# Where tiles start in SBUF: moving every TensorE operand to a multiple of 256 bytes

## The chip, the cores and the metric

The kernel runs on one core of a Trainium2 chip. The metric is the device time of one execution in microseconds (us), as the median of several runs. TensorE (PE) multiplies; its weight loads are shown as a row of their own (PEld). VectorE is DVE, ScalarE is ACT, GpSimd is POOL, and SyncE (SP) issues the DMAs. SBUF is the on-chip memory that all engines read; an address below is an offset in bytes within a partition of SBUF.

## The reference

An encoder of four layers works on 256 tokens of width 1024. Layer i has one token mixer (i mod 3), then a dense SwiGLU layer; each half is normalised before and after.

```
for i in range(4):
    hn = rmsnorm(x, norm_w[i, 0])
    m = [retention, conv_module, dilated_attention][i % 3](hn, ...)
    x = x + rmsnorm(m, norm_w[i, 1])
    a = rmsnorm(x, norm_w[i, 2]) @ ffn_w_in[i]            # 1024 -> 2 * 2816
    x = x + rmsnorm((silu(a[:, :2816]) * a[:, 2816:]) @ ffn_w_out[i], norm_w[i, 3])
```

So the mixers are retention, conv, attention and retention again. Nearly all the arithmetic is products of a 256-token activation with a weight matrix in float32.

## The kernel before

The tokens are held as two tiles of 128 (t = 0 and t = 1). Each float32 factor of a product is split in two parts of type float32r, a high part `h` and the rest `l`, and a product is made of three matmuls: h·h, h·l and l·h. A weight block of 128 x 1024 arrives by DMA in `raw`; ACT casts it to `wh` (L50) and DVE makes `wl` by a subtraction (L51). Ten such pairs rotate in the pool `wp`.

`proj` (L181) multiplies an activation with four weight blocks: 24 matmuls into one PSUM bank. The *moving* operand, the one that streams through the array, is a 512-column slice of `wh` or `wl` (384 columns in attention). The *stationary* operand, which a weight load puts into the array beforehand, is a 128-column block of the transposed activation, `xTh0`/`xTl0` for t = 0 and `xTh1`/`xTl1` for t = 1. Every matmul comes with its own weight load.

`out_block` (L198; L188 in its other order) makes the products with an output matrix. In the SwiGLU layer its moving operands are `poolh`/`pooll` and its stationary ones `fhh`/`fhl`; in retention they are `wh`/`wl` and `rh`/`rl`. `mix` of retention (L322) has `vh`/`vl` moving and `ph`/`pl` stationary. `taps` of the conv layer (L575) multiplies 256 columns of `upad` with diagonal blocks `dg` in plain float32. Transposes (L160, L457, L693 and others) are PE instructions too.

The SwiGLU layer goes through 11 groups of 256 hidden columns. For group c the order on PE is up(0, c+1), down(0, c), a transpose, up(1, c), down(1, c-1), a transpose, where up is `proj` and down is 12 matmuls of `out_block`.

Where a tile lies is not written anywhere in the code. Pools take space one behind the other in the order of the code, and each tile starts at the next multiple of 32 bytes after the one before. A tile of 4 or 8 bytes per partition thus moves all that lies behind it by 32 bytes. The small tiles ahead of and between the large ones are `nhalf` (4 bytes), two pairs of `rsx` (8 bytes each), six `ss`, six `rs`, `bn`, `lnm`, `asc` and `warm`.

Of the kernel before, what the change touches and what calls it, by code (L numbers as in the profile page):

```python
# [8 lines left out]
F32 = mybir.dt.float32  # L9
F32R = mybir.dt.float32r  # L10
AF = mybir.ActivationFunctionType
# [3 lines left out]
P = 128  # L15
D = 1024
KB = 8
# [3 lines left out]
PAIRS = 8  # L21
# [16 lines left out]
def tile_trunk(ctx: ExitStack, tc: tile.TileContext, a):  # L38
    nc = tc.nc

    const = ctx.enter_context(tc.tile_pool(name="const", bufs=1))
    wp = ctx.enter_context(tc.tile_pool(name="wp", bufs=WBUFS))
    work = ctx.enter_context(tc.tile_pool(name="work", bufs=2))
# [32 lines left out]
        with tc.issue_after(cast[0].ins), tc.issue_after(cast[1].ins):  # L76
            yield

# [1 line left out]
    xs = [const.tile([P, D], F32, tag=f"x{t}", name=f"x{t}") for t in range(2)]  # L80
    grow = work.tile([1, D], F32, tag="gain", name="grow", bufs=2)
    nc.sync.dma_start(grow, a["norm_w"][0:1, :])
# [6 lines left out]
    gain0 = [bank("acc"), bank("acc")]  # L89
    for hh in range(2):  # L90
        nc.tensor.matmul(gain0[hh], lhsT=ones, rhs=grow[:, hh * 512 : hh * 512 + 512], start=True, stop=True)
    nhalf = const.tile([P, 1], F32, tag="nhalf", name="nhalf")
    nc.vector.memset(nhalf, -0.5)

    xTh, xTl = [None, None], [None, None]

# [5 lines left out]
    def rsqrt_mean(ss0, ss1, eps, scale=None, keep=None):  # L102
        if keep is None:
            r = work.tile([P, 2], F32, tag="rs", name="rs", bufs=6)
        else:
            r = const.tile([P, 2], F32, tag=f"rsx{keep}", name="rsx", bufs=2)
        if scale is None:
            nc.gpsimd.tensor_scalar(r[:, 0:1], ss0, ss1, eps, op0=ALU.add, op1=ALU.add)  # L108
        else:
            nc.gpsimd.tensor_scalar(r[:, 0:1], ss0, scale, eps, op0=ALU.mult, op1=ALU.add)  # L110
        nc.gpsimd.tensor_tensor(out=r[:, 1:2], in0=r[:, 0:1], in1=nhalf, op=ALU.pow)
        return r[:, 1:2]
# [20 lines left out]
    rsx = {}  # L133
# [69 lines left out]
                    stop=(last and i == 2),  # L203
                )

# [1 line left out]
    def retention_decay(j, pool):  # L207
        tmp = pool
        dist = work.tile([P, 2, 512], F32, tag="fg", name="dist", bufs=1)
        nc.sync.dma_start(dist, a["ret_dist"])  # L210
        lm = tmp.tile([P, 8], F32, tag="lm", name="lm")
        nc.sync.dma_start(lm, a["log1m"][j : j + 1, :].partition_broadcast(P))
        ebase = tmp.tile([P, 8], F32, tag="ebase", name="ebase")
        nc.vector.memset(ebase, math.e)
        ex = tmp.tile([P, 8], F32, tag="ex", name="ex")
        nc.gpsimd.tensor_tensor(out=ex, in0=ebase, in1=lm, op=ALU.pow)
        gm = tmp.tile([P, 8], F32, tag="gm", name="gm")
        nc.vector.tensor_scalar(gm, ex, -1.0, 1.0, op0=ALU.mult, op1=ALU.add)
        lg = tmp.tile([P, 8], F32, tag="lg", name="lg")
        nc.scalar.activation(lg, gm, AF.Ln)  # L220
        dts = []
        for h in range(RET_HEADS):
            dt = pool.tile([P, 512], F32, tag=f"dt{j}_{h}", name=f"dt{j}_{h}", bufs=1)
            nc.vector.tensor_scalar_mul(dt, dist[:, 0, :], lg[:, h : h + 1])
            nc.vector.scalar_tensor_tensor(
                out=dt, in0=dist[:, 1, :], scalar=lg[:, 4 + h : 5 + h], in1=dt, op0=ALU.mult, op1=ALU.add
            )
            nc.scalar.activation(dt, dt, AF.Exp)
            dts.append(dt)
        return dts  # L230

# [1 line left out]
    def retention(j, gload, decay, finish, pool, first):  # L233
        dts = []
        rope = pool.tile([P, 2, 2, P], F32, tag="rope", name="rope", bufs=1)
# [274 lines left out]
        finish(1, acc[1])  # L510

    def conv(j, finish, pool, prefetch):
        chv = pool.tile([P, 5, KB], F32, tag="chv", name="chv", bufs=1)
        nc.sync.dma_start(chv, a["conv_ch"][j])
        wdw = pool.tile([P, KB, TAPS], F32, tag="wdw", name="wdw", bufs=1)
        nc.sync.dma_start(wdw, a["conv_w_dw"][j])
        bout = pool.tile([P, D], F32, tag="cbout", name="cbout", bufs=1)
# [4 lines left out]
        cvp = pool.tile([P, KB, 256], F32, tag="cvp", name="cvp", bufs=1)  # L522

        def perm(v):
            # natural token 4 u + r, read as (r, u)
            return v.rearrange("p (u r) -> p r u", r=4)

        def glu(t, c, ws, mid=None):
# [74 lines left out]
        with tc.issue_after(last_tap["v"].ins):  # L603
            wo = [load_w(a["conv_w_out"][j, k]) for k in range(CONV_EARLY)]
        yh, yl = {}, {}
        warm = pool.tile([P, 1], F32, tag="warm", name="warm", bufs=1)
        with tc.issue_after(last_tap["a"].ins):
            nc.scalar.activation(warm, nhalf, AF.Silu)
        for t in range(2):
            bs = [bank("acc"), bank("acc")]  # L610
            bn = work.tile([P, 2, 6], F32, tag="bn", name="bn", bufs=2)
            ms = work.tile([P, 4], F32, tag="lnm", name="lnm", bufs=2)
            for hh in range(2):
                for k in range(4):
                    nc.tensor.transpose(
                        bs[hh][:, k * P : (k + 1) * P], cvp[:, 4 * hh + k, t * P : (t + 1) * P], ident
                    )
                nc.vector.bn_stats(bn[:, hh, :], bs[hh])
            nc.vector.bn_aggr(ms[:, 0:2], bn)
            rs = rsqrt_mean(ms[:, 1:2], None, LN_EPS, scale=1.0)  # L620
            nc.vector.tensor_scalar(ms[:, 2:3], ms[:, 0:1], rs, -1.0, op0=ALU.mult, op1=ALU.mult)
            yc = pool.tile([P, D], F32, tag="yc", name="yc", bufs=1)
            nc.vector.tensor_scalar(yc[:, 0:512], bs[0], ms[:, 0:1], rs, op0=ALU.subtract, op1=ALU.mult)
            nc.scalar.activation(yc[:, 512:1024], bs[1], AF.Identity, scale=rs, bias=ms[:, 2:3])
            h = const.tile([P, KB, P], F32R, tag=f"xTh{t}", name=f"yh{t}")
            l = const.tile([P, KB, P], F32R, tag=f"xTl{t}", name=f"yl{t}")
            for hh in range(2):
                tp = bank("aux")
                sy = pool.tile([P, 4, P], F32, tag="sy", name="sy", bufs=2)
                for k in range(4):  # L630
                    cb = 4 * hh + k
                    nc.tensor.transpose(tp[:, k * P : (k + 1) * P], yc[:, cb * P : (cb + 1) * P], ident)
                for k in range(4):
                    cb = 4 * hh + k
                    nc.scalar.activation(
                        sy[:, k, :],
                        tp[:, k * P : (k + 1) * P],
                        AF.Silu,
                        scale=chv[:, 1, cb : cb + 1],
                        bias=chv[:, 2, cb : cb + 1],  # L640
                    )
                ends = split(
                    h[:, 4 * hh : 4 * hh + 4, :].rearrange("p k t -> p (k t)"),
                    l[:, 4 * hh : 4 * hh + 4, :].rearrange("p k t -> p (k t)"),
                    sy.rearrange("p k t -> p (k t)"),
                )
                if t == 0 and hh == CONV_FENCE:
                    with tc.issue_after(ends[0].ins), tc.issue_after(ends[1].ins):
                        wo += [load_w(a["conv_w_out"][j, k]) for k in range(CONV_EARLY, KB)]
                        prefetch()  # L650
            yh[t], yl[t] = h, l
# [191 lines left out]
        outp(1, range(4, KB))  # L843
        finish(1, acc[1])

# [1 line left out]
    pre_norm(0, gain0, late=True)  # L847

    for i in range(DEPTH):
        kind, j = i % 3, i // 3  # L850
        gains = {}

        def finish(t, f):
            post_norm(t, f, gains[0])
            pre_norm(t, gains[1])
# [27 lines left out]
            ffn(i, finish_ffn, pool)  # L883


# [1 line left out]
def _layout(inputs):  # L887
    import numpy as np

    f32 = np.float32  # L890
    pos = np.arange(256)
    tok = 4 * (pos % 64) + pos // 64
# [10 lines left out]
    w = inputs["ret_w_in"]  # L903
    nr = w.shape[0]
    qk = w[:, :, : 2 * D].reshape(nr, D, 2, RET_HEADS, 256).transpose(0, 3, 1, 2, 4).reshape(nr, RET_HEADS, 1, D, 512)
    vg = w[:, :, 2 * D :].reshape(nr, D, 2, RET_HEADS, 512).transpose(0, 3, 2, 1, 4)
    w = np.concatenate([qk, vg], axis=2)
# [4 lines left out]
    w = inputs["conv_w_in"]  # L912
    n = w.shape[0]
# [4 lines left out]
    chv = [inputs[k].reshape(n, 1, KB, P) for k in ("conv_b_dw", "conv_ln_g", "conv_ln_b")]  # L918
# [3 lines left out]
    c["conv_b_out"] = inputs["conv_b_out"]  # L922
    w = inputs["attn_w_in"]
    n = w.shape[0]
    w = w.reshape(n, D, 3, 3, PAIRS, 2, 64)  # group, qkv, pair, head of pair, dim
    qk = w[:, :, :, 0:2].transpose(0, 4, 3, 1, 5, 2, 6)  # n pair qk D head group dim
    g0 = qk[:, :, :, :, :, 0].reshape(n, PAIRS, 2, D, 128)
    g12 = qk[:, :, :, :, :, 1:3].reshape(n, PAIRS, 2, D, 256)
    qk = np.concatenate([g0, g12], axis=4)
    v = w[:, :, :, 2].transpose(0, 3, 1, 2, 4, 5).reshape(n, PAIRS, 1, D, 384)  # L930
    w = np.concatenate([qk, v], axis=2)
# [1 line left out]
        w.reshape(n, PAIRS, 3, 4, 2, P, 384).transpose(0, 1, 2, 3, 5, 4, 6).reshape(n, PAIRS, 3, 4, P, 768)  # L933
    )
    c["attn_w_out"] = inputs["attn_w_out"].reshape(n, KB, P, D)
    # tables of positions only
    tf = tok.astype(f32)
    diff = tok[None, :] - tok[:, None]  # query n minus key m, [m, n]
    dist = np.stack([np.maximum(diff, 0), np.maximum(-diff, 0)]).astype(f32)  # 2, m, n
    c["ret_dist"] = dist.reshape(2, 2, P, 256).transpose(2, 0, 1, 3).reshape(P, 2, 512)  # L940
    inv = (1.0 / (f32(10000.0) ** np.linspace(0.0, 1.0, 128, dtype=f32))).astype(f32)
    ang = tf[:, None] * inv[None, :]
# [36 lines left out]
```

## Time and profile before

| | |
|---|---|
| median of three runs | 1625.04 us (1624.56 to 1625.5) |
| span of the profiled execution, first to last instruction | 1623.5 us |
| PE busy | 1604.0 us (99%), 7742 matmuls and transposes |
| PEld busy | 1345.9 us |
| DVE busy | 1038.4 us (64%) |
| ACT busy | 864.0 us (53%) |
| DMA | 274 MB, mean 169 GB/s |
| mean granted TensorE clock | 0.997 of full speed (2.4 GHz) |

The profiled execution has no time of its own beside its span; the median of the timed runs is 1.5 us longer than the span, which is what lies around the first and last instruction. Matmuls are pipelined, so the busy time of PE says only that it never ran dry. How fast it goes is read from the distance between the starts of two matmuls that follow each other.

### The profile page before, as it was taken

Reading aid. Unit: us, or ns where it says so; the run is one execution under the profiler, and the core shown is the slowest. Engines: PE = TensorE matmul, PEld = TensorE weight load, DVE = VectorE, ACT = ScalarE, POOL = GpSimd, SP = SyncE. Lnnn points to the kernel's source line nnn. Section 1 sums busy time; section 2 is a strip of 40 time slices with the busy share of each in tenths; the row PEclk is TensorE's granted clock in tenths of the full one; section 3 lists DMA queues with packets and bytes.
Section 4 is the critical chain, followed back from the end, with each engine's and each line's share of the span. In section 5 each row is a group of like instructions: output and inputs, shape, how many; then the busy total and the mean of one; then the engine's idle time right before and its main releaser. Section 6 shows DMA issues by size and latency. Waiting matters only on the chain.

```text
span 1623.5 us, 20999 instructions
## 1 busy us (share of the span) xinstructions
PE 1604.0 (99%) x7742; PEld 1345.9 (83%) x7742; DVE 1038.4 (64%) x1576; ACT 864.0 (53%) x1376; POOL 69.8 (4%) x106
## 2 busy tenths in 40 slices
PE   9999999999999999999999999999999999999998
PEld 6888878888787788889999999788888888878886
DVE  7755685546797854557777767755567655675452
ACT  7544464445687644546656656644456444555341
POOL 1000010001000100010000000100010000010000
PEclk9999999999999999999999999999999999999999
DMA  8645474655304755544444444564655543475530
GB/s 316 234 137 178 156 244 171 203 185 182 121 1 145 254 200 179 169 131 142 153 147 131 143 143 156 202 213 168 205 174 169 180 167 127 160 238 194 194 117 26
DMA packets 79882, 274.27 MB, mean 169 GB/s; under 512 B 9378, under 2 KB 9634, under 8 KB 79779
## 3 DMA queue, kind: packets, MB, share of 16 engines
q1 hardware_dynamic: 79778, 272.92, 49.7%
q8 instruction: 61, 1.00, 0.2%
q14 instruction: 43, 0.34, 0.1%
HBM read 271.84 MB, written 1.05 MB: 168 GB/s over the span
## 4 chain that ended last, share of the span: by engine, by line
PE 91%; DVE 3%; ACT 2%; DMA 2%; issue 1%; POOL 0%; SPq 0%; DVEq 0%; POOLq 0%; ACTq 0%
PE mm L181 58%; PE acc L198 20%; PE acc L575 3%; PE aux L322 1%; PE acc L772 1%; PE aux L457 1%; DMA raw<-in_ffn_w_out 1%; PE acc L731 1%; PE acc L729 1%; PE aux L757 1%; DVE wl L51 1%; ACT junk L116 1%; PE aux L298 1%; DMA raw<-in_ffn_w_in 1%; PE aux L693 1%
## 5 line engine op out<-in xcount | busy, mean ns | idle before, releaser
L181 PE MATMUL mm<-wh,xTh 128*128 128x512 f32 (+1 forms) x1536 | 596.8, 389 | 0.8 <-ACT xTh L50 0.8
L181 PE MATMUL mm<-wh,xTl 128*128 128x512 f32 (+1 forms) x1536 | 583.1, 380 | 0.0
L181 PE MATMUL mm<-wl,xTh 128*128 128x512 f32 (+1 forms) x1536 | 582.6, 379 | 0.0
L51 DVE TENSOR_TENSOR wl<-raw,wh 128x1024 fp32r<-128x1024 f32 (+1 forms) x432 | 497.5, 1163 | 118.9 <-ACT wh L50 107.9
L50 ACT CAST wh<-raw 128x1024 fp32r<-128x1024 f32 (+1 forms) x432 | 429.1, 1003 | 141.7 <-PE mm L181 107.8
L181 PEld LDWEIGHTS mm<-wh,xTl 128*128 128x128 f32 x1536 | 289.1, 188 | 50.2 <-DVE xTl L51 0.3
L181 PEld LDWEIGHTS mm<-wl,xTh 128*128 128x128 f32 x1536 | 289.8, 189 | 44.5 <-DVE wl L51 0.5
L181 PEld LDWEIGHTS mm<-wh,xTh 128*128 128x128 f32 x1536 | 289.3, 188 | 44.8 <-ACT xTh L50 1.2
L446 ACT ACTIVATE fsg<-mm,rsx 128x256 f32<-128x256 f32 x88 | 41.7, 473 | 171.6 <-PE mm L181 171.6
L448 DVE SCALAR_TENSOR_TENSOR fsg<-mm,rsx,fsg 128x256 f32<-128x256 f32 x88 | 42.3, 481 | 127.7 <-ACT fsg L446 127.5
L51 DVE TENSOR_TENSOR pooll<-raw,poolh 128x1024 fp32r<-128x1024 f32 x88 | 107.4, 1222 | 9.2 <-ACT poolh L50 7.9
L198 PE MATMUL acc<-poolh,fhh 128*128 128x512 f32 x344 | 108.6, 396 | 0.5 <-ACT fhh L50 0.5
L198 PE MATMUL acc<-poolh,fhl 128*128 128x512 f32 x344 | 107.3, 392 | 0.0
L198 PE MATMUL acc<-pooll,fhh 128*128 128x512 f32 x344 | 107.1, 393 | 0.0
L50 ACT CAST poolh<-raw 128x1024 fp32r<-128x1024 f32 x88 | 92.2, 1049 | 26.7 <-PE acc L198 15.4
L51 DVE TENSOR_TENSOR fhl<-aux,fhh 128x256 fp32r<-128x256 f32 x88 | 37.0, 421 | 98.4 <-ACT fhh L50 98.4
L50 ACT CAST fhh<-aux 128x256 fp32r<-128x256 f32 x88 | 32.5, 369 | 115.6 <-PE aux L457 115.6
L198 PEld LDWEIGHTS acc<-pooll,fhh 128*128 128x128 f32 x344 | 64.6, 188 | 14.5
L198 PEld LDWEIGHTS acc<-poolh,fhh 128*128 128x128 f32 x344 | 63.7, 188 | 15.4 <-ACT fhh L50 2.7
L198 PEld LDWEIGHTS acc<-poolh,fhl 128*128 128x128 f32 x344 | 64.3, 188 | 14.6
L559 DVE SCALAR_TENSOR_TENSOR cv<-upad,wdw,cv 128x256 f32<-128x256 f32 x143 | 59.5, 479 | 0.8
L108 POOL TENSOR_SCALAR rs<-ss 128x1 f32<-128x1 f32 x16 | 7.5, 468 | 1061.5 <-ACT junk L116 1061.5
(178 smaller groups left out, 1617.2 us busy)
## 6 DMA issues: line engine op xcount, KB each, us to landing
raw<-in_ffn_w_in SPq DMA_DIRECT2D x176, 512.0 KB, 4.8
raw<-in_ret_w_in SPq DMA_DIRECT2D x96, 512.0 KB, 4.6
raw<-in_ffn_w_out SPq DMA_DIRECT2D x88, 512.0 KB, 4.4
raw<-in_attn_w_in SPq DMA_DIRECT2D x96, 384.0 KB, 3.7
raw<-in_ret_w_out SPq DMA_DIRECT2D x32, 512.0 KB, 4.7
raw<-in_conv_w_in SPq DMA_DIRECT2D x16, 512.0 KB, 4.6
gain<-in_norm_w SPq DMA_DIRECT2D x15, 512.0 KB, 5.2
raw<-in_conv_w_out SPq DMA_DIRECT2D x8, 512.0 KB, 4.0
```

The source lines that it names most:

```text
L50: ia = nc.scalar.copy(h, src)
L51: iv = nc.vector.tensor_sub(l, src, h.bitcast(F32))
L116: nc.scalar.activation(junk, src, AF.Square, scale=scale, accum_out=acc)
L181: nc.tensor.matmul(out, lhsT=st[t][:, k, :], rhs=mv[:, sl], start=(n == 0), stop=(n == 23))
L198: nc.tensor.matmul(acc[hh], lhsT=st, rhs=mv[:, hh * 512 : hh * 512 + 512], start=(first and i == 0), stop=(last and i == 2),)
L298: nc.tensor.matmul(b[:, m * 256 : (m + 1) * 256], lhsT=kt[:, 2 + half, m * P : (m + 1) * P], rhs=qt[:, half, :], start=(n == 0), stop=(n = ...
L322: nc.tensor.matmul(b, lhsT=pt[:, m, t * P : (t + 1) * P], rhs=vt[:, m, :], start=(n == 0), stop=(n == 5))
L446: nc.scalar.activation(sg, b[:, 0:256], AF.Silu, scale=rsx[t])
L448: nc.vector.scalar_tensor_tensor(out=sm, in0=b[:, 256:512], scalar=rsx[t], in1=sg, op0=ALU.mult, op1=ALU.mult)
L457: nc.tensor.transpose(tp[:, k * P : (k + 1) * P], sm[:, k * P : (k + 1) * P], ident)
L559: last_tap["v"] = nc.vector.scalar_tensor_tensor(out=cv, in0=upad[:, cb, w : w + 256], scalar=wdw[:, cb, w : w + 1], in1=cv, op0=ALU.mult, ...
L575: nc.tensor.matmul(pc[:, 0:256], lhsT=dgs[w], rhs=upad[:, cb, w : w + 256], start=(w == 0), stop=(w == TAPS - 1),)
```

## The change

No instruction is added or taken away and none has other elements to work on. Six small tiles are made wider, with the added elements never read; `nhalf` is allocated first and set first. On PE, ACT, POOL and SP the instructions stand in the same order as before.

```
-    nhalf = const.tile([P, 1], F32, tag="nhalf", name="nhalf")
-    nc.vector.memset(nhalf, -0.5)
+    nhalf_t = const.tile([P, 32], F32, tag="nhalf", name="nhalf")
+    nc.vector.memset(nhalf_t, -0.5)
+    nhalf = nhalf_t[:, 0:1]
...
-            r = const.tile([P, 2], F32, tag=f"rsx{keep}", name="rsx", bufs=2)
+            r = const.tile([P, 32], F32, tag=f"rsx{keep}", name="rsx", bufs=2)
...
-        lg = tmp.tile([P, 8], F32, tag="lg", name="lg")
-        nc.scalar.activation(lg, gm, AF.Ln)
+        lg = tmp.tile([P, 32], F32, tag="lg", name="lg")
+        nc.scalar.activation(lg[:, 0:8], gm, AF.Ln)
...
-        chv = pool.tile([P, 5, KB], F32, tag="chv", name="chv", bufs=1)
-        nc.sync.dma_start(chv, a["conv_ch"][j])
+        chv = pool.tile([P, 9, KB], F32, tag="chv", name="chv", bufs=1)
+        nc.sync.dma_start(chv[:, 0:5, :], a["conv_ch"][j])
...
-        warm = pool.tile([P, 1], F32, tag="warm", name="warm", bufs=1)
+        warm = pool.tile([P, 64], F32, tag="warm", name="warm", bufs=1)
...
-            ms = work.tile([P, 4], F32, tag="lnm", name="lnm", bufs=2)
+            ms = work.tile([P, 16], F32, tag="lnm", name="lnm", bufs=2)
```

What it moves are addresses. This table has the start of each operand of PE in the built programs, as the remainder of its address by 256. The last column but one is the start of the moving operand less that of the stationary one, by 256, before the change; the last is the same after it. Columns within a tile are cut at multiples of 512 bytes and change nothing in it; the 256-column slices of `upad` start at every fourth byte.

| line, moving with stationary | moving before | stationary before | all after | difference before | after |
|---|---|---|---|---|---|
| L181, t = 0: `wh`, `wl` with `xTh0`, `xTl0` | 32 | 160 | 0 | 128 | 0 |
| L181, t = 1: `wh`, `wl` with `xTh1`, `xTl1` | 32 | 224 | 0 | 64 | 0 |
| L198, L188 SwiGLU: `poolh`, `pooll` with `fhh`, `fhl` | 224 | 224 | 0 | 0 | 0 |
| L198 retention: `wh`, `wl` with `rh`, `rl` | 32 | 32 | 0 | 0 | 0 |
| L322: `vh`, `vl` with `ph`, `pl` | 224 | 32 | 0 | 192 | 0 |
| L198 attention: `wh`, `wl` with `oh`, `ol` | 32 | 224 | 0 | 64 | 0 |
| L198 conv: `wh`, `wl` with `yh0`, `yh1` and rests | 32 | 160, 224 | 0 | 128, 64 | 0 |
| the 256-column products of L298, L729, L731, L772 | 224 | 224 | 0 | 0 | 0 |

Before the change, then, every float32r operand started 32 bytes past a multiple of 64.

The one instruction that changes its place is a memset at the start of DVE's program. Before, DVE begins like this (`ones` is the row of ones with which PE spreads the first gain over the partitions, `ebase` a constant of the retention decay):

```order
L88 MEMSET ones 1x128
L93 MEMSET nhalf 128x1
L214 MEMSET ebase 128x8
L139 TENSOR_TENSOR xg<-x_67,acc 128x512 x2
L51 TENSOR_TENSOR wl<-raw,wh 128x1024
```

After the change the same place reads:

```order
L82 MEMSET nhalf 128x32
L92 MEMSET ones 1x128
L216 MEMSET ebase 128x8
L141 TENSOR_TENSOR xg<-x_69,acc 128x512 x2
L51 TENSOR_TENSOR wl<-raw,wh 128x1024
```

`nhalf` went ahead of `ones` and has 32 columns in place of 1; everything behind them is as it was, four engines included.

## Rows read from the trace of the kernel before

**Rows 1.** The page: span, busy time of PE, and the chain that ended last.

```profile
span 1623.5 us, 20999 instructions
PE 1604.0 (99%) x7742; PEld 1345.9 (83%) x7742; DVE 1038.4 (64%) x1576; ACT 864.0 (53%) x1376; POOL 69.8 (4%) x106
...
PE 91%; DVE 3%; ACT 2%; DMA 2%; issue 1%; POOL 0%; SPq 0%; DVEq 0%; POOLq 0%; ACTq 0%
```

**Rows 2.** Waits of PE: who waited for whom, total us, times, longest us.

```profile
PE aux L457 <- DVE fsg L448: 3.4, 3, 1.6
PE aux L632 <- DVE yc L623: 2.6, 1, 2.6
PE acc L91 <- DMA grow<-in_norm_w: 2.3, 1, 2.3
```

**Rows 3.** Timeline of PE in the first SwiGLU layer: start us, duration us, instruction.

```profile
313.44 0.40 PE L181 MATMUL mm<-wl,xTh 128*128 128x512 f32 x1
...
318.71 0.63 PE L198 MATMUL acc<-poolh,fhh 128*128 128x512 f32 x2
...
321.48 0.38 PE L457 MATMUL aux<-ident,fsg 128*128 128x128 f32 x2
...
321.94 0.39 PE L181 MATMUL mm<-wl,xTh 128*128 128x512 f32 x1
...
327.27 0.62 PE L198 MATMUL acc<-poolh,fhh 128*128 128x512 f32 x2
...
330.01 0.38 PE L457 MATMUL aux<-ident,fsg 128*128 128x128 f32 x2
```

**Rows 4.** Timeline of PE in retention, output product (first and last of 24).

```profile
56.24 0.62 PE L198 MATMUL acc<-wh,rh 128*128 128x512 f32 x2
...
61.68 0.49 PE L343 MATMUL aux<-ident,go 128*128 128x128 f32 x3
```

**Rows 5.** Timeline of PE in retention: `mix`, then a `proj` of t = 1.

```profile
187.10 0.39 PE L322 MATMUL aux<-vh,ph 128*128 128x512 f32 x1
...
189.89 0.40 PE L181 MATMUL mm<-wh,xTh 128*128 128x512 f32 x1
...
192.46 0.40 PE L181 MATMUL mm<-wh,xTl 128*128 128x512 f32 x1
```

**Rows 6.** Timeline of PE in attention: 384 columns, t = 0, then t = 1.

```profile
812.72 0.34 PE L181 MATMUL mm<-wl,xTh 128*128 128x384 f32 x1
...
816.77 0.49 PE L693 MATMUL aux<-ident,ar 128*128 128x128 f32 x3
...
817.27 0.34 PE L181 MATMUL mm<-wl,xTh 128*128 128x384 f32 x1
...
821.09 0.34 PE L181 MATMUL mm<-wh,xTl 128*128 128x384 f32 x1
```

**Rows 7.** Groups by line and shape: count, busy us, mean ns, idle before.

```profile
L181 PE MATMUL mm<-wh,xTh 128*128 128x512 f32 x1152 | 464.6, 403 | 0.8 <-ACT xTh L50 0.8
...
L181 PE MATMUL mm<-wh,xTh 128*128 128x384 f32 x384 | 132.2, 345 | 0.0
L198 PE MATMUL acc<-poolh,fhh 128*128 128x512 f32 x344 | 108.6, 396 | 0.5 <-ACT fhh L50 0.5
...
L198 PE MATMUL acc<-wh,rh 128*128 128x512 f32 x128 | 40.0, 393 | 0.0
...
L322 PE MATMUL aux<-vh,ph 128*128 128x512 f32 x32 | 12.6, 395 | 0.0
```

**Rows 8.** Conv taps in plain float32: timeline of PE, then their group.

```profile
459.64 4.70 PE L575 MATMUL acc<-upad,dg 128*128 128x256 f32 x21
...
L575 PE MATMUL acc<-upad,dg 128*128 128x256 f32 x200 | 43.5, 378 | 0.0
```

**Rows 9.** Windows: us, busy PE, PEld, DVE, ACT, POOL, clock, DMA share, GB/s.

```profile
10.00:25.00 15.00, 15.00 (x65) 12.26 (x65) 14.51 (x21) 10.73 (x18) 4.33 (x5) 1.00 0.98 374
210.00:228.00 18.00, 17.28 (x80) 13.85 (x79) 15.64 (x21) 12.96 (x21) 3.74 (x6) 1.00 0.91 299
290.00:390.00 100.00, 100.00 (x448) 81.41 (x447) 51.30 (x59) 44.78 (x59) 0.00 (x0) 1.00 0.54 183
...
900.00:1000.00 100.00, 100.00 (x625) 96.56 (x624) 73.59 (x172) 62.77 (x120) 0.00 (x0) 1.00 0.45 146
```

More of the change, by code (lines that the diff above doesn't have):

```diff
@@ L605, in conv @@
         yh, yl = {}, {}
-        warm = pool.tile([P, 1], F32, tag="warm", name="warm", bufs=1)
+        warm = pool.tile([P, 64], F32, tag="warm", name="warm", bufs=1)
         with tc.issue_after(last_tap["a"].ins):
-            nc.scalar.activation(warm, nhalf, AF.Silu)
+            nc.scalar.activation(warm[:, 0:1], nhalf, AF.Silu)
         for t in range(2):
```

## The prediction, before the changed kernel was run

> **What bounds the kernel now.** First the page: PE is busy for 1604.0 of 1623.5 us and takes 91% of the chain that ended last [rows 1]. Next the waits of PE, to see whether anything starves it: the longest entries are 3.4, 2.6 and 2.3 us in total [rows 2], so all its waits together are about 1%. The kernel is therefore as long as PE's stream of matmuls, and a change that adds and removes no instruction can act only through how closely they follow each other. That is the third view, the timeline of PE: the start of the first matmul of a run, the start of what follows the run, and the count between.
>
> Two SwiGLU runs that differ only in their stationary tile do not have the same pace [rows 3]. For t = 1, from 313.44 to 318.71 us there are 23 steps: 5.27 / 23 = 229.1 ns. For t = 0, from 321.94 to 327.27, again 23: 5.33 / 23 = 231.7 ns. (The first matmul of each run is left out, since it still carries the switch from the transposes.) The `down` runs of 12 behind them take 2.77 / 12 = 230.8 and 2.74 / 12 = 228.3 ns, mean 229.6. The output product of retention is the quickest, 5.44 / 24 = 226.7 ns [rows 4], and `mix` the slowest, 2.79 / 12 = 232.5 ns [rows 5]. With 384 columns t = 0 takes 4.05 / 23 = 176.1 ns and t = 1 takes 3.82 / 22 = 173.6 ns [rows 6].
>
> Set these beside the table of addresses. By the difference of the two starts: 0 gives 226.7 (retention) and a mean of 229.6 in the short `down` runs; 64 gives 229.1; 128 gives 231.7; 192 gives 232.5. Shape, type and engine are the same in all of them. I read this as the streaming read of one matmul and the weight load of the next, which runs beside it, getting in each other's way in SBUF, by an amount that hangs on how their addresses stand to each other. That is an inference; the ordering is what the rows show.
>
> A floor can be read too. A plain float32 tap counts 256 columns and the trace has it as one of two halves, each 4.70 us less a last duration of 0.38, over 20 steps: 216 ns [rows 8]. Against this the quickest float32r matmul of 512 columns, at 226.7, is 10.7 ns longer. In the taps the start of the moving slice walks along in steps of 4 bytes.
>
> **The change, part by part.** Everything is at remainder 0 afterwards, so every difference is 0. If the difference is what counts, all float32r matmuls of 512 columns go to the pace of [rows 4]. Counts are from the groups [rows 7]; each has three products, and L181 is shared evenly by t = 0 and t = 1.
>
> - L181, 512 columns, t = 0: 3 x 1152 / 2 = 1728, each 231.7 - 226.7 = 5.0 ns: 8.6 us.
> - L181, 512 columns, t = 1: 1728 x 2.4 ns: 4.1 us.
> - SwiGLU `down`: 3 x 344 by the row (24 more stand at L188), 1056 in all, x 2.9 ns: 3.1 us. Their difference is 0 already; the gain comes from no longer having to recover from the slower pattern of the `up` run ahead.
> - `mix`: 96 x 5.8 ns: 0.6 us.
> - L181, 384 columns, t = 0: 576 x 2.5 ns: 1.4 us.
> - The output products of attention and conv: 192 matmuls at differences of 64 and 128, so 2.4 to 5.0 ns each: 0.5 to 1.0, I take 0.6 us.
>
> Sum: 18.4 us at most for this mechanism. At the other end the whole stream could behave as the `down` runs do now, difference 0 but 229.6 ns because a run is too short to settle: then t = 0 gives 1728 x 2.1 = 3.6 us, t = 1 loses 1728 x 0.5 = 0.9, and some 3.5 us are left with the small terms. I take 16 us, near the upper end, since [rows 4] shows a run at 226.7 from its first matmul although a t = 0 run stands right ahead of it, and since after the change no neighbour has another difference.
>
> The rest costs nothing, with its cover. The wider memset of `nhalf` ahead of `ones` delays PE's first matmul only if it outlasts the 2.3 us wait for the gain's DMA [rows 2]; 31 more columns cannot, and without that cover it would be part of a microsecond. No DMA is added and none carries more bytes. DVE, ACT and the DMAs get other addresses as well. The trace shows no other address to price that by; a shorter DVE or ACT instruction gives nothing, since DVE is busy 51 and ACT 45 of 100 us in the SwiGLU stretch and 74 and 63 in attention [rows 9]. Quicker landings would help only where loads are the limit, 10 to 25 us and 210 to 228 us, at 98% and 91% DMA share; PE is idle there for 0.7 us, so from 0 to about 1 us. The same slack lets the gain through: a PE that is 1% or even 5% faster needs DVE at 78% at most.
>
> The profiled execution's span is 1623.5 us and the median 1625.0; the 1.5 us around the span do not change. Forecast: 1625.0 - 16 = **1609 us**, with a range of its own from 1606 to 1621.
>
> **The rivals.** *A: it is the half-line start itself that costs.* Every float32r operand began 32 bytes past a multiple of 64. If the 10.7 ns above the floor are a partial fetch at the start of each operand, they go too: another 10.7 ns on 5184 + 1152 = 6336 matmuls, 68 us, with the 18.4 us together 86: 1539 us. If half of it goes, 34 us: 1573. For it: the taps, with the same 512 steps of the array, lack these 10.7 ns. Against it: they lack them at all starts, also 32 bytes past a multiple of 64, and a plain float32 tap has time to spare for its reads, so they cannot decide. Chance 0.25, half of it below 1558.
> The Trainium skill (TensorE: Matmul & The Clock Gate, Back-to-back issue gap) gives the distance of two matmuls as columns over 2.4 GHz plus 2.5 ns, 216 ns for 512; the taps' 216 agrees, and by that rule alone the time would be rival A's.
>
> *B: nothing happens.* The pattern may be set by history, not by address. After `mix` at 187 us a `proj` of t = 1 runs at 2.57 / 11 = 233.6 ns [rows 5], though the same pair of addresses takes 229.1 elsewhere [rows 3]: it kept the pattern of the run ahead. If each run is only handed the pace of the one before, with nothing that pulls it to its own, the time stays: 1625 us. Against it: t = 0 and t = 1 return to their own pace in every SwiGLU group. Chance 0.09.
> The Trainium skill (SBUF — State Buffer, Specifications) has engine accesses go by lines of 16 bytes. Every start was a multiple of 32 before, so by this rule none was split and the change does nothing; that the pace differs between t = 0 and t = 1 at starts that all meet the rule speaks against it here.
>
> *C: slower.* With everything at remainder 0, each matmul's stream and the next one's weight load start at the same remainder, always. If that remainder is a bad one and all runs lock into the slow pattern at 232.5 ns [rows 5], t = 0 loses 0.8 x 1728 = 1.4, t = 1 3.4 x 1728 = 5.9, `down` 2.9 x 1056 = 3.1 and the retention output 5.8 x 384 = 2.2 us: 12.6 us, 1638. It decides from a mean of 230.0 ns, which is what the runs now have, weighted by their counts. Against it: equal starts at 32 and at 224 both reach the quickest pattern. Chance 0.08.
>
> **How the numbers follow.** Forecast 0.58, A 0.25, B 0.09, C 0.08. Faster is the forecast and A, 0.83; same is B, 0.09; slower is C, 0.08. About 0.2% (3 us) is what a measurement of this kernel can tell from no change. The time is the forecast's, 1609. The range leaves out A's full form (half of A, 0.12) and C (0.08): from 1558, below A's half form with some room, to 1627, just above B.
>
> **What would show it.** Right: `up` runs of t = 0 and t = 1 at one pace near 227 ns, `down` the same from its first matmuls, `mix` near 227, 384 columns near 173.5 for both, and the retention output unchanged at 226.7. Rival A shows in that last run: anything clearly below 226 there means that the absolute start counts. B shows t = 0 and t = 1 still apart by 2.6 ns. C shows the retention output above 230. The forecast is wrong if paces fall but the span does not, which would need PE waits that are not in [rows 2].

## The result, and the profile after

The median went from 1625.04 us to **1612.1 us** (five runs of each; 1624.56 to 1625.5 before, 1612.01 to 1616.1 now), a ratio of 0.9926 with an interval of 0.9914 to 0.9939. The profiled execution took 1612.1 us, of which its span is 1610.3 us: 13.2 us less than before, with the same 20999 instructions and the same mean clock of 0.997. Lines of the helpers moved by two: L183 is the former L181, L200 the former L198, L324 the former L322, and so on.

The page of the changed kernel, span, busy time and the chain that ended last (the lines that answer to [rows 1]):

```profile
span 1610.3 us, 20999 instructions
PE 1589.4 (99%) x7742; PEld 1344.2 (83%) x7742; DVE 1038.5 (64%) x1576; ACT 864.4 (54%) x1376; POOL 71.3 (4%) x106
...
PE 90%; ACT 3%; DVE 2%; DMA 2%; issue 1%; POOL 1%; SPq 0%; DVEq 0%; POOLq 0%; ACTq 0%
```

PE's busy time fell by 14.6 us; DVE and ACT are where they were. The waits of PE (waiting for whom, total us, times, longest us; compare [rows 2]):

```profile
PE aux L459 <- DVE fsg L450: 2.8, 3, 1.7
PE aux L634 <- DVE yc L625: 2.6, 1, 2.6
PE acc L95 <- DMA grow<-in_norm_w: 2.5, 1, 2.5
PE aux L459 <- issue: 1.6, 1, 1.6
```

The first three are the old ones. The fourth is in the load-limited stretch around 220 us, where the windows view now reads (us, then busy PE, PEld, DVE, ACT, POOL, clock, DMA share, GB/s; compare [rows 9]):

```profile
210.00:228.00 18.00, 16.38 (x77) 13.25 (x77) 16.15 (x20) 11.84 (x20) 2.97 (x4) 1.00 0.86 300
```

PE is idle there for 18.00 - 16.38 = 1.62 us, where it was 0.72: 0.9 us of the gain went into this wait, and the loads come at 300 GB/s as before (299). The profile names no releaser ("issue"), but the timeline does: the transposes need `fsg`, whose ACT instruction stands behind a cast that waits for its load, 1.32 us now and 0.65 before.

Now the distances, on the timeline of PE in the first SwiGLU layer of the changed kernel (start us, duration us, instruction; compare [rows 3]). The first two rows bound a t = 1 run, the second and third the `down` run behind it; the last four rows are the same for t = 0, with one matmul from its middle.

```profile
311.55 0.39 PE L183 MATMUL mm<-wl,xTh 128*128 128x512 f32 x1
...
316.78 0.61 PE L200 MATMUL acc<-poolh,fhh 128*128 128x512 f32 x2
...
319.51 0.38 PE L459 MATMUL aux<-ident,fsg 128*128 128x128 f32 x2
...
319.96 0.39 PE L183 MATMUL mm<-wl,xTh 128*128 128x512 f32 x1
...
321.34 0.39 PE L183 MATMUL mm<-wl,xTh 128*128 128x512 f32 x1
...
325.20 0.62 PE L200 MATMUL acc<-poolh,fhh 128*128 128x512 f32 x2
...
327.92 0.38 PE L459 MATMUL aux<-ident,fsg 128*128 128x128 f32 x2
```

For t = 1: 5.23 / 23 = 227.4 ns; for t = 0: 5.24 / 23 = 227.8 ns. The 2.6 ns between them are gone. The `down` runs take 2.73 / 12 = 227.5 and 2.72 / 12 = 226.7. The middle row shows what is left over: the first 6 steps of the t = 0 run take 1.38 / 6 = 230.0 ns, the 17 after them 3.86 / 17 = 227.1.

Retention in the changed kernel: the output product, 24 matmuls, then `mix` and the `proj` of t = 1 behind it (compare [rows 4] and [rows 5]).

```profile
150.60 0.62 PE L200 MATMUL acc<-wh,rh 128*128 128x512 f32 x2
...
156.05 0.38 PE L345 MATMUL aux<-ident,go 128*128 128x128 f32 x2
...
186.16 0.39 PE L324 MATMUL aux<-vh,ph 128*128 128x512 f32 x1
...
188.88 0.39 PE L183 MATMUL mm<-wh,xTh 128*128 128x512 f32 x1
...
191.38 0.39 PE L183 MATMUL mm<-wh,xTl 128*128 128x512 f32 x1
```

The output product stands at 5.45 / 24 = 227.1 ns, as before within the 10 ns to which such rows are printed. `mix` went from 232.5 to 2.72 / 12 = 226.7, and the `proj` that held the slow pattern behind it from 233.6 to 2.50 / 11 = 227.3.

384 columns in attention, t = 1 and then t = 0 (compare [rows 6]):

```profile
802.92 0.34 PE L183 MATMUL mm<-wl,xTh 128*128 128x384 f32 x1
...
806.91 0.49 PE L695 MATMUL aux<-ident,ar 128*128 128x128 f32 x3
...
807.42 0.34 PE L183 MATMUL mm<-wl,xTh 128*128 128x384 f32 x1
...
811.41 0.49 PE L695 MATMUL aux<-ident,ar 128*128 128x128 f32 x3
```

3.99 / 23 = 173.5 and 3.99 / 23 = 173.5 ns: one pace for both.

### The profile page after: what moved, and what is told of

The parts are those of the page before. It is cut to its first block, busy times and chain, and to the rows that moved or that the text cites. A ratio compares the mean times of both kernels' runs of the same rounds, so it can differ in the third digit from the quotient of the medians.

```text
span 1610.3 us, 20999 instructions
## 1 busy us (share of the span) xinstructions
PE 1589.4 (99%) x7742; PEld 1344.2 (83%) x7742; DVE 1038.5 (64%) x1576; ACT 864.4 (54%) x1376; POOL 71.3 (4%) x106
## 4 chain that ended last, share of the span: by engine, by line
PE 90%; ACT 3%; DVE 2%; DMA 2%; issue 1%; POOL 1%; SPq 0%; DVEq 0%; POOLq 0%; ACTq 0%
PE mm L183 57%; PE acc L200 21%; PE acc L577 3%; PE acc L774 1%; PE aux L459 1%; PE aux L324 1%; PE acc L733 1%; PE acc L731 1%; PE aux L759 1%; ACT wh L50 1%; ACT junk L118 1%; DMA raw<-in_ffn_w_out 1%; DVE wl L51 1%; PE aux L300 1%; PE aux L695 1%
## 5 line engine op out<-in xcount | busy, mean ns | idle before, releaser
L183 PE MATMUL mm<-wh,xTh 128*128 128x512 f32 (+1 forms) x1536 | 591.1, 385 | 1.2 <-ACT xTh L50 1.2
L183 PE MATMUL mm<-wl,xTh 128*128 128x512 f32 (+1 forms) x1536 | 579.4, 377 | 0.0
L183 PE MATMUL mm<-wh,xTl 128*128 128x512 f32 (+1 forms) x1536 | 579.2, 377 | 0.0
L183 PEld LDWEIGHTS mm<-wh,xTl 128*128 128x128 f32 x1536 | 288.8, 188 | 45.8 <-DVE xTl L51 0.3
L183 PEld LDWEIGHTS mm<-wh,xTh 128*128 128x128 f32 x1536 | 289.0, 188 | 43.4 <-ACT xTh L50 1.6
L183 PEld LDWEIGHTS mm<-wl,xTh 128*128 128x128 f32 x1536 | 289.4, 188 | 41.9 <-DVE wl L51 0.5
L200 PE MATMUL acc<-poolh,fhh 128*128 128x512 f32 x344 | 107.6, 393 | 0.5 <-ACT fhh L50 0.5
L200 PE MATMUL acc<-poolh,fhl 128*128 128x512 f32 x344 | 107.2, 392 | 0.0
L200 PE MATMUL acc<-pooll,fhh 128*128 128x512 f32 x344 | 106.0, 389 | 0.0
L50 ACT CAST poolh<-raw 128x1024 fp32r<-128x1024 f32 x88 | 92.6, 1054 | 24.2 <-PE acc L200 14.6
L200 PEld LDWEIGHTS acc<-poolh,fhh 128*128 128x128 f32 x344 | 63.7, 188 | 15.1 <-ACT fhh L50 2.7
L200 PEld LDWEIGHTS acc<-pooll,fhh 128*128 128x128 f32 x344 | 64.6, 188 | 13.5
L200 PEld LDWEIGHTS acc<-poolh,fhl 128*128 128x128 f32 x344 | 64.3, 188 | 13.5
```

The costliest lines, as they stand in the source:

```text
L50: ia = nc.scalar.copy(h, src)
L183: nc.tensor.matmul(out, lhsT=st[t][:, k, :], rhs=mv[:, sl], start=(n == 0), stop=(n == 23))
L200: nc.tensor.matmul(acc[hh], lhsT=st, rhs=mv[:, hh * 512 : hh * 512 + 512], start=(first and i == 0), stop=(last and i == 2),)
```

## The experiments

All times below are of kernels that compute the whole layer stack, unless the text says otherwise; the kernel before ran beside them at 1625.35 us (the first three) and 1625.33 us (the two on `rsx`).

**Is it the multiple of 256?** Here `nhalf` is 32 bytes longer, so that every tile behind it moves by 32: all operands start at remainder 32 and all differences stay 0.

```
-    nhalf_t = const.tile([P, 32], F32, tag="nhalf", name="nhalf")
+    nhalf_t = const.tile([P, 40], F32, tag="nhalf", name="nhalf")
```

> All tiles start 32 bytes later than after the change: every start at remainder 32, every difference 0. If only the difference counts: 226.7 ns settled everywhere, 1612 us (1610 to 1615). If the absolute start counts (a multiple of 256, or of 64): the gain is lost in part or whole, 1617 to 1625 us, and settled runs go above 228 ns.

Measured: 1612.05 us (1610.98 to 1613.15), ratio to the kernel before 0.9922 (0.9908 to 0.9935), the same as the change. A t = 0 run of this kernel on the timeline of PE:

```profile
319.82 0.39 PE L183 MATMUL mm<-wl,xTh 128*128 128x512 f32 x1
...
325.06 0.61 PE L200 MATMUL acc<-poolh,fhh 128*128 128x512 f32 x2
```

5.24 / 23 = 227.8 ns, to the digit what the changed kernel has. No operand lies at a multiple of 256 or even of 64 here, and nothing is lost. What this kernel shares with the changed one is the difference of 0 in every pair. Rival A falls: the half-line start costs nothing.

**One difference put back.** `rsx` has 64 bytes in place of 128. That moves `xTh1` and `xTl1` (and with them `yh1` and `yl1` of the conv output, 48 matmuls) to remainder 128 and leaves all else at 0: t = 1 has now the difference that t = 0 had before.

```
-            r = const.tile([P, 32], F32, tag=f"rsx{keep}", name="rsx", bufs=2)
+            r = const.tile([P, 16], F32, tag=f"rsx{keep}", name="rsx", bufs=2)
```

> Every start is a multiple of 128, but xTh1 and xTl1 lie at remainder 128, so L183 runs of t = 1 have a difference of 128 and all others 0. If the difference counts: t = 1 runs near 231.7 ns as t = 0 runs were before, t = 0 at 226.7; 1728 x (231.7 - 227.8) = 6.7 us and about 1.5 us in the products behind them, 1619 to 1621 us. If the absolute start counts: 1612 us.

Measured: 1621.08 us (1619.63 to 1623.16), ratio 0.9977 (0.9968 to 0.9985). Its timeline, a t = 1 run, the `down` run behind it, and the t = 0 run that follows:

```profile
312.47 0.39 PE L183 MATMUL mm<-wl,xTh 128*128 128x512 f32 x1
...
317.81 0.62 PE L200 MATMUL acc<-poolh,fhh 128*128 128x512 f32 x2
...
320.57 0.38 PE L459 MATMUL aux<-ident,fsg 128*128 128x128 f32 x2
...
321.02 0.39 PE L183 MATMUL mm<-wl,xTh 128*128 128x512 f32 x1
...
326.26 0.62 PE L200 MATMUL acc<-poolh,fhh 128*128 128x512 f32 x2
```

t = 1 takes 5.34 / 23 = 232.2 ns, t = 0 5.24 / 23 = 227.8. The slow pace follows the difference, not the tile or its place in the program. The `down` run behind t = 1 has difference 0 itself and takes 2.76 / 12 = 230.0 ns, against 227.5 in the changed kernel. Nothing but the run ahead is different here, so some of its slowness reaches into the next run.

**A slow difference for both t.** With `ones` 64 bytes longer and the second `rsx` pair at 96 bytes, the transposed activations of both t start at 64, so that L183 (L184 here) has the difference 192 throughout, and with it the 96 matmuls of the conv output; everything else is at 0.

```
-    ones = const.tile([1, P], F32, tag="ones", name="ones")
-    nc.vector.memset(ones, 1.0)
+    ones_t = const.tile([1, P + 16], F32, tag="ones", name="ones")
+    nc.vector.memset(ones_t, 1.0)
+    ones = ones_t[:, 0:P]
...
-            r = const.tile([P, 32], F32, tag=f"rsx{keep}", name="rsx", bufs=2)
+            r = const.tile([P, 32 if keep == 0 else 24], F32, tag=f"rsx{keep}", name="rsx", bufs=2)
```

> Every start is a multiple of 64, xT tiles of both t at remainder 64: a difference of 192 for all of L183, 0 elsewhere. If the difference counts: 232 to 234 ns in L183 as in mix before, 3456 x (232.5 - 227.8) = 16 us and 2 to 3 us behind, 1629 to 1633 us, slower than the kernel before. If a start at a multiple of 64 is what counts: 1612 us.

Measured: 1630.23 us (1629.47 to 1632.0), ratio 1.0034 (1.0022 to 1.0047): slower than the kernel before, although every operand starts at a multiple of 64. A run of t = 0 with its `down` run:

```profile
324.09 0.40 PE L184 MATMUL mm<-wl,xTh 128*128 128x512 f32 x1
...
329.46 0.62 PE L201 MATMUL acc<-poolh,fhh 128*128 128x512 f32 x2
...
332.20 0.38 PE L460 MATMUL aux<-ident,fsg 128*128 128x128 f32 x2
```

5.37 / 23 = 233.5 ns, and `down` 2.74 / 12 = 228.3. Between this kernel and the change lie 18.1 us for 3456 matmuls, 5.2 ns each; the two L183 paces differ by 233.5 - 227.6 = 5.9.

**The price list.** This kernel computes no layer; it copies `x` to the output and runs groups of 30 matmuls that differ only in the starts `m` and `s` of their operands (in floats), each followed by four transposes. It was run once, for its distances.

```
    def group(m, s, width=512, cols=128, count=30, m2=None, s2=None, mt=None, st=None):
        ...
            nc.tensor.matmul(
                b[0:cols, 0:width],
                lhsT=st[:, so : so + cols],
                rhs=mt[:, mo : mo + width],
                start=(n == 0),
                stop=(n == count - 1),
            )
```

> No layer is computed: groups of 30 matmuls of one pair of starts each, in one PSUM bank, with four transposes between groups; the output is the input x. If the difference by 256 counts: 226.7 ns at differences 0, 256 and 512, about 229 at 64, 231.7 at 128, 232.5 or more at 192, equal for equal differences whichever operand is moved, and 226.7 for both at 32, 64 or 128. Between float32r matmuls with 64 or 32 stationary columns, if the weight load of the next matmul is what the stream meets, the distance falls below 226.7 (towards 216), and bfloat16 has 216 at every start. If every third matmul has another stationary start, the interval of the matmul ahead of it is the long one, not its own.

Measured, as the mean of the last twelve distances of a group (512 columns, float32r):

| moving less stationary, by 256 | 0 | 32 | 64 | 96 | 128 | 160 | 192 | 224 |
|---|---|---|---|---|---|---|---|---|
| stationary at 0, moving shifted (ns) | 226.7 | 233.3 | 228.9 | 233.3 | 232.5 | 234.2 | 233.3 | 233.3 |
| moving at 0, stationary shifted (ns) | 226.7 | 233.3 | 228.9 | 233.3 | 232.6 | 234.2 | 233.3 | 233.3 |

Shifts of 256 and 512 give 226.7 again, and so do both operands at 32, 64 or 128 together. Whichever operand is shifted, the difference alone gives the price. On the timeline of PE, groups with the differences 128, 192 and 0 (both at 32), then one in bfloat16, each with the transposes that end it:

```profile
54.77 7.21 PE L87 MATMUL mm<-mv,sv 128*128 128x512 f32 x30
61.82 0.60 PE L78 MATMUL aux<-ident,raw 128*128 128x128 f32 x4
...
69.65 7.25 PE L87 MATMUL mm<-mv,sv 128*128 128x512 f32 x30
76.74 0.60 PE L78 MATMUL aux<-ident,raw 128*128 128x128 f32 x4
...
217.54 7.08 PE L87 MATMUL mm<-mv,sv 128*128 128x512 f32 x30
224.46 0.60 PE L78 MATMUL aux<-ident,raw 128*128 128x128 f32 x4
...
310.65 6.64 PE L87 MATMUL mm<-mb,sb 128*128 128x512 bf16 x30
317.13 0.60 PE L78 MATMUL aux<-ident,raw 128*128 128x128 f32 x4
```

From start to transposes: 7.05, 7.09, 6.92 and 6.48 us for 30. Over its last twelve distances bfloat16 takes 215.8 ns, with the difference 0 and with 128 alike. Further: 256 columns take 120.0 ns at difference 0 and 118.4 at 128; 384 columns 173.3 and 175.7; with 64 columns in the stationary operand the pace is 230.0 (difference 0) and 231.2 (128), with 32 columns 231.7. The weight loads of 64 and 32 columns last 134 and 109 ns in this trace, those of 128 columns 189. Had the weight load that runs beside the stream been what costs, a shorter one should not have made the pace slower: here the inference of the prediction lost its first support. In one more group every third matmul had its stationary operand at 128. Expected was that the interval of the matmul ahead of it is the long one; over the last 24 the one ahead takes 232.4 ns, its own 234.2 and the third 226.8, so that both are long. The same with the moving operand at 128 gives 231.1 in the mean, without a clear order.

**Mixed groups, fewer columns, other differences.** Again no layer is computed. Groups alternate float32r (F) and bfloat16 (B) matmuls, step the difference by 32 with 256 and 384 columns, and narrow the stationary operand.

```
+            mt, st = (mv, sv) if kinds[n % len(kinds)] == "F" else (mb, sb)
...
+    for kinds in ("FB", "FFB", "FBB", "FFFFB"):
+        group(0, 0, kinds=kinds)
+        group(32, 0, kinds=kinds)
...
+        for m in (0, 8, 16, 24, 32, 40, 48, 56):
+            group(m, 0, width=w)
...
+    for k in (4, 1, 2, 3, 4):
+        group(0, 0, mark=k)
```

> Groups of matmuls as before, no layer computed, the output is the input x. F is a float32r matmul, B a bfloat16 one, both of 512 columns, in turn in one group. If what lengthens F is the weight load of the next float32r matmul beside its stream: F followed by B takes about 216 ns and F followed by F 226.7, so FB has a mean of 216, FFB one of 219.5, FFFFB one of 224, and the difference of starts matters only where F follows F. If the 10.7 ns are F's own, whatever comes next: FB 221, FFB 223, FFFFB 224.5, and F is longer by 10.7 ns in each. Fewer stationary columns: the theory of the next load said shorter, the first groups were longer (230 and 231.7); a scan over starts shows whether some start brings them to 226.7 or below. 256 and 384 columns: 0 is the quickest start if the rule of equal starts holds for all widths; 118.4 at 128 against 120.0 at 0 in the first groups of 256 speaks against it there. Runs behind 1, 2, 3 or 4 transposes: if the first ten matmuls of a run are slow because of the phase that the transposes leave, their sum changes with the number.

Measured: FB alternating takes 230.0 ns in the mean (231.7 at difference 128), more than either kind alone, so the switch of type has a price of its own and these groups decide nothing. Stationary operands of 96, 64 and 32 columns take from 228.3 to 233.3 ns at every difference tried, none below the 226.7 of 128 columns. Behind one to four transposes, a group at difference 0 needs 6 to 10 matmuls to reach 226.7, and the number of transposes makes no clear difference. With 256 columns difference 0 is not the quickest; the groups at 0 and at 32 on the timeline of PE:

```profile
90.50 3.84 PE L84 MATMUL mm<-mv,sv 128*128 128x256 f32 x30
94.18 0.60 PE L78 MATMUL aux<-ident,raw 128*128 128x128 f32 x4
94.54 3.75 PE L84 MATMUL mm<-mv,sv 128*128 128x256 f32 x30
98.12 0.60 PE L78 MATMUL aux<-ident,raw 128*128 128x128 f32 x4
```

3.68 and 3.58 us for 30; settled, 120.0 ns at difference 0 and 116.7 at 32. With 384 columns the differences 0, 32, 64, 160 and 224 all take 173.3 ns, and 96, 128 and 192 take 176.4 to 176.7. Which differences are slow thus hangs on the number of columns.

**Which edit does it?** The kernel before with `rsx` alone widened. All of L181's operands then lie at remainder 160; `mix` keeps its difference of 192 and the attention output its 64.

```
-            r = const.tile([P, 2], F32, tag=f"rsx{keep}", name="rsx", bufs=2)
+            r = const.tile([P, 32], F32, tag=f"rsx{keep}", name="rsx", bufs=2)
```

> The kernel before with rsx 128 bytes wide and nothing else: xTh0, xTl0, xTh1, xTl1, wh and wl all start at remainder 160, so L181 has a difference of 0 for both t with no start a multiple of 64. mix (192) and the attention output (64) keep their differences. If only differences count: all of the gain but 96 x 5.8 ns and 96 x 2.4 ns, so 1612.1 + 0.8 = 1613 us (1611 to 1615). If starts at multiples of 256 add anything: 1616 or more.

Measured: 1613.99 us (1612.02 to 1616.07), ratio 0.993 (0.9918 to 0.9943). A t = 0 run:

```profile
320.81 0.39 PE L181 MATMUL mm<-wl,xTh 128*128 128x512 f32 x1
...
326.04 0.62 PE L198 MATMUL acc<-poolh,fhh 128*128 128x512 f32 x2
```

5.23 / 23 = 227.4 ns. One line gives 11.3 us, nearly all of the gain.

**And all the others without it.** The changed kernel with `rsx` back at `[P, 2]`: every operand at a multiple of 64, L183 (and the conv output) at the differences 128 and 64, everything else at 0.

```
-            r = const.tile([P, 32], F32, tag=f"rsx{keep}", name="rsx", bufs=2)
+            r = const.tile([P, 2], F32, tag=f"rsx{keep}", name="rsx", bufs=2)
```

> The changed kernel with rsx at 8 bytes again: differences in L183 are 128 for t = 0 and 64 for t = 1 as before the change, every start a multiple of 64, all other pairs at 0. If only differences count: 1625 - 0.8 = 1624 us (1622 to 1626), settled runs at 232 and 229 ns. If starts at multiples of 64 count: below 1618.

Measured: 1622.63 us (1621.9 to 1623.84), ratio 0.9985 (0.9976 to 0.9994). Its t = 1 run, then its t = 0 run, each with its `down` run:

```profile
313.75 0.40 PE L183 MATMUL mm<-wl,xTh 128*128 128x512 f32 x1
...
319.03 0.62 PE L200 MATMUL acc<-poolh,fhh 128*128 128x512 f32 x2
...
321.75 0.38 PE L459 MATMUL aux<-ident,fsg 128*128 128x128 f32 x2
...
322.21 0.39 PE L183 MATMUL mm<-wl,xTh 128*128 128x512 f32 x1
...
327.55 0.62 PE L200 MATMUL acc<-poolh,fhh 128*128 128x512 f32 x2
...
330.29 0.38 PE L459 MATMUL aux<-ident,fsg 128*128 128x128 f32 x2
```

5.28 / 23 = 229.6 and 5.34 / 23 = 232.2 ns, the paces of [rows 3]. The five other widenings give 2.7 us. The `down` runs take 2.72 / 12 = 226.7 and 2.74 / 12 = 228.3 ns, though the runs ahead of them are as slow as before the change; before, the first of them took 230.8. Added up over the whole trace, the distances of the SwiGLU output are 246.6 us in the kernel before, 243.2 here, 243.8 with `rsx` alone and 243.0 after the change.

**Whose difference, and which starts?** No layer is computed here either. Two kinds of matmul alternate, so that a matmul's own difference can be told from that of its stream against the next one's weight load; and both operands start at 8 to 112 bytes.

```
+            m, s = starts[n % len(starts)]
...
+        group((0, 0), (d, d), count=42)
+        group((0, d), (d, 0), count=42)
...
+    for x in (2, 4, 6, 8, 12, 24, 28):
+        group((x, x))
+    for d in (16, 32, 48):
+        group((4, 4 + d))
```

> Groups of matmuls again, no layer computed, the output is the input x. A group takes turns between two pairs of starts (moving, stationary), in remainders. (0, 0) and (128, 128) in turn: each stream has its own stationary start as its own, and the next one's at a difference of 128. (0, 128) and (128, 0) in turn: the other way round. If the stream meets the weight load of the next matmul: the first takes 232 ns and the second 226.7. If the start of its own stationary operand counts: 226.7 and 232. The same for 64 and 192 with 229 and 233. Four in turn, as 0, 64, 128, 192 in step: 226.7 where the rule's difference is 0 in each. Both starts at 8, 16, 24, 32, 48, 96 or 112 bytes: 226.7 only at multiples of 32.

Measured, mean ns of the settled part, starts as (moving, stationary) in bytes: (0, 0) with (64, 64) 231.7, (0, 64) with (64, 0) 231.7; (0, 0) with (128, 128) 228.4, (0, 128) with (128, 0) 230.0; (0, 0) with (192, 192) 231.4, (0, 192) with (192, 0) 233.3. If only a matmul's own difference counted, the first of each pair would be 226.7; if only that against the next weight load counted, the second of each pair would be. Neither holds, so the rule between neighbours stays open. Four starts in turn, equal in each matmul (0, 64, 128, 192), take 230.5 ns, where 226.7 was expected, and a group at (0, 0) and (192, 0) in turn takes 226.7, although every second matmul of it has a difference of 192. The two groups with 128, and last a group at (16, 208), on the timeline of PE:

```profile
65.76 9.85 PE L84 MATMUL mm<-mv,sv 128*128 128x512 f32 x42
75.44 0.60 PE L78 MATMUL aux<-ident,raw 128*128 128x128 f32 x4
75.80 9.91 PE L84 MATMUL mm<-mv,sv 128*128 128x512 f32 x42
85.55 0.60 PE L78 MATMUL aux<-ident,raw 128*128 128x128 f32 x4
...
243.39 7.05 PE L84 MATMUL mm<-mv,sv 128*128 128x512 f32 x30
250.29 0.60 PE L78 MATMUL aux<-ident,raw 128*128 128x128 f32 x4
```

9.68 and 9.75 us for 42. Both operands at 32 or 96 take 226.7 ns; both at 8, 16, 24, 48 or 112 take 231.1 to 233.3. Of the equal starts tried, only those at multiples of 32 reach 226.7. They are not the only quick pair: with the moving operand at 16 and the stationary one at 208 the group takes 6.90 us for 30 and settles at 226.7 ns too, while 16 with 80 takes 228.9 and 16 with 144 takes 233.3. As far as tried, the difference alone gives the price only for starts at multiples of 32.

## Why the prediction was right, and where its gain was too large

The measured 1612.1 us lie in the forecast's own range of 1606 to 1621, 3.1 us above its 1609.

**The bound** was read rightly: PE's stream is the kernel's length, and 13.2 us less of span go with 14.6 us less of busy PE. **The reading of [rows 3] to [rows 5]**, that the pace hangs on the difference of the two starts, held for `proj` with 512 columns in every kernel that computes the layers: moved as one block nothing changes (1612.05), one difference put back costs 9.0 us, a bad difference for all 18.1 us, and the groups of 30 give the four prices that were read (226.7, 228.9, 232.5, 233.3 against 226.7, 229.1, 231.7, 232.5).

**The terms.** The trace's start-to-start distances, added up over all matmuls of a line in both kernels:

| term | before, us | after, us | gain | forecast |
|---|---|---|---|---|
| L181, 512 columns, with what follows each run | 816.2 | 807.9 | 8.3 | 8.6 + 4.1 = 12.7 |
| SwiGLU output | 246.6 | 243.0 | 3.6 | 3.1 |
| 384 columns | 205.6 | 204.6 | 1.0 | 1.4 |
| `mix` | | | 0.6 | 0.6 |
| other outputs | | | 0.1 | 0.6 |
| sum | | | 13.6 | 18.4, of which 16 taken |

The term that was mis-sized is the first. It priced every L181 matmul at 226.7 ns, the pace of a run that follows another run of matmuls [rows 4]. But a `proj` run mostly stands behind transposes, and needs 5 to 10 matmuls to settle: the 3137 distances within the runs fell from a mean of 231.4 to 228.3 ns, not to 226.7. That is 3.1 x 3137 = 9.7 us (the first distance of each run gave 0.4 more). The paces taken from the two runs of [rows 3], 231.7 and 229.1 ns, have a mean of 230.4, so the start was read 1.0 ns too quick and the end 1.6. The rest went into waits behind the runs, which grew by 1.8 us, the one at 220 us by 0.9 alone; the prediction had noted that stretch as load-limited with 0.7 us of idle PE, and did not price it as a place where a part of the gain is lost. The deduction from 18.4 to 16 was meant for runs too short to settle and was too small: 18.4 less 4.8 was right.

The **`down` term**, a gain for runs whose own difference never changed, came out at 3.6 us against 3.1 (1.2 of it in the steps from the last matmul of a run to what follows, waits included), but its reason does not hold as it was given. It was to come from `up` runs that are no longer slow. Already in [rows 3] the slower `down` run (230.8 ns) stands behind the quicker `up` run (229.1). And the kernel with all widenings but `rsx` has `up` runs as slow as before, and yet a SwiGLU output of 243.2 us, which is 3.4 of the 3.6 us (within the runs alone 1.8 of 2.4). A run ahead can slow `down`, as 230.0 ns behind t = 1 at 128 shows; but behind a t = 0 run of the same pace (232.2) and the same difference it takes 228.3 in the kernel without the wide `rsx`. That the term came out near its size is in part luck, and what sets the pace of `down` stays open.

**The costs put at nothing** were nothing. The wait for the gain's DMA is 2.5 us after the change and 2.2 us in the kernel without the wide `rsx`, which has the same wide memset of `nhalf` (the one instruction that works on more elements than before); so the memset does not set it. DVE's and ACT's busy times moved by 0.1 and 0.4 us.

**The rivals.** A fell twice: the retention output stayed at 227, and a kernel with every operand 32 bytes past a multiple of 64 is as quick. The Trainium skill (TensorE: Matmul & The Clock Gate, Back-to-back issue gap) gives 216 ns for 512 columns as the gap of a single matmul, and about 131 ns for a stream of weight loads and matmuls. The trace agrees with the first for bfloat16 (215.8 ns, each matmul with its own weight load) and not for float32r, whose best is 226.7 ns; the second was seen nowhere. B fell with the two paces of [rows 3], now 227.4 and 227.8, and with the `proj` behind `mix`, now 227.3. The Trainium skill (SBUF — State Buffer, Specifications (TRN2)) counts lines of 16 bytes; all starts are multiples of 32 in the kernels of 1612.05, 1622.63 and 1630.23 us, so that rule does not tell them apart and the measurement decides. C needed 232.5 ns at equal starts, and they reach 226.7.

**The mechanism behind the ordering** was called an inference, and it stays one. A stream that meets the next matmul's weight load would suffer less from a narrower weight load, and with 96, 64 or 32 stationary columns the pace was never below 226.7; alternating starts fitted neither a matmul's own difference nor the one against its neighbour. The runs show which differences are slow at 512 columns; why they are, and what the 10.7 ns are that float32r takes over the taps at the best difference, stays open.

## What to carry to other kernels

Where float32r matmuls follow each other without waits, compare the start-to-start distance of runs that differ only in their operands; if they differ by 2 to 7 ns, look at where the moving and the stationary tile start by 256 bytes. At 512 columns what paid here was the same remainder for both operands, at a multiple of 32 bytes, and not that it is zero. Other pairs can be as quick, and at 384 and 256 columns other differences are slow, so measure the pair and the width that the kernel has. Neighbours of different starts cost as well: groups that alternate between two equal pairs take 228.4 to 231.7 ns. One small tile of odd size between two large ones can set all this for the whole kernel: here one line gave 11.3 of 13 us. When pricing such a gain, take the mean over runs of the length and neighbours that the kernel has, not the settled pace.

## What was not expected of the hardware

- The difference costs from 2.2 ns (64) to 7.5 ns (160) in a distance of 226.7 ns at 512 columns in float32r, and nothing in bfloat16 at the two differences tried (215.8 at 0 and at 128).
- Starts that are equal but no multiple of 32 bytes are slow too: 233.3 ns with both at 16. Unequal ones can be quick: 226.7 ns with 16 and 208.
- With 256 columns the order turns: 120.0 ns at difference 0, 116.7 at 32. The 256-column products of retention and attention stand at 0, and moving them was not tried. An estimate from these two figures, 3.3 ns on all 480 of them, is 1.6 us, 0.1% of the time.
- A stationary operand of fewer columns is not quicker: 230.0 ns with 64 columns and 231.7 with 32, against 226.7 with 128.
